# Token halves change roles in the block scheme of the up projection, and the first tile's S1 T1 and A22 T4 are issued early

## The chip, the cores and the metric

The kernel runs on one core of one Trainium2 chip. The metric is the device time of one execution in microseconds (us); the median of three runs before the change is 2224.79 us (2224.76 to 2225.38).

## The reference

Two layers of an encoder trunk on 1024 tokens of width 1024, float32. What matters here is the end of each layer:

```
x  = x + concat(A, B, C) @ W_out
h2 = rmsnorm(x)
up = dwconv3(h2 @ ffn_w_up)            # 1024 -> 2 * 2816
gate, val = split(up)
x  = x + (silu(gate) * val) @ ffn_w_down
```

`A`, `B`, `C` are the outputs of attention, of spatial gating and of a short gated convolution; `dwconv3` is a depthwise convolution over three neighbouring tokens.

## The kernel before

Float32 products are made of three products each: every operand is split into a high part (a rounded copy, on ScalarE) and a low part (the rest, a subtraction on VectorE or GpSimd), and high x high, high x low and low x high are summed in PSUM (`split`, line 114). A product of 128x128 weights with 512 columns is one TensorE instruction; twelve of them (four chunks of the inner dimension, three each) are one *group* (`block_mm`, line 862).

**The up projection** computes 22 tiles (`up_tile`, line 888), each of 128 gate and 128 value channels for all 1024 tokens. A tile is a 2x2 block product by Winograd's scheme with seven products instead of eight. The activations h2 are cut into A11, A12 (two halves of the inner dimension, first 512 tokens) and A21, A22 (the same, last 512 tokens); the weights into B11, B12, B21, B22. From them S1 = A21 + A22, S2 = S1 - A11, S3 = A11 - A21, S4 = A12 - S2 and T1 = B12 - B11, T2 = B22 - T1, T3 = B22 - B12, T4 = T2 - B21 are formed (some with their sign turned). The seven products are A11 B11, A12 B21, S1 T1, S2 T2, S3 T3, S4 B22 and A22 T4. Three of them run on in one PSUM bank u (A11 B11, S2 T2, S3 T3, and A22 T4 behind them), and copies (`cp`, ScalarE) and adds (`add`, line 902, VectorE) take partial sums out of u in between: p1 after the first, u1 after the second. c2 holds A12 B21, c5 holds S1 T1 (copied out as p5) and S4 B22.

**How h2 gets there.** For each of eight blocks of 128 tokens, `norm2_step` (line 815) issues the second half of the output projection (`out_proj`, line 734: five splits on ScalarE and GpSimd, 24 products, and the sum with x on VectorE, line 756), stores x, normalizes the block before (`norm_a`: the square on ScalarE, two short GpSimd operations, the scaling on VectorE at line 262) and issues `norm2_b` (line 770) for the block before that: eight transposes on TensorE into a pair of PSUM banks (line 774), and from there the operand parts. For blocks 0 to 3 these are a copy of both halves (line 783) and the splits of A11 and A12; for blocks 4 to 7 the split of A22, S3 and S2 on VectorE (lines 790, 791) and the two sums for S1 and S4 on GpSimd (lines 792, 793). When all eight blocks are done, `norm2_end` (line 795) splits S2, S1, S3 and S4: ScalarE copies and VectorE subtractions of 128x1024 elements. The PSUM pairs (`big`) are two, of the bank kinds `pa` there are two, of `po` and `pf` one.

**The order.** The program is scheduled by the compiler's expected times (line 1289), except in `manual_schedule` sections, where VectorE, GpSimd and ScalarE keep the written order and TensorE is still scheduled. One such section (lines 1187 to 1205) covers the passage from the last blocks to the first tile. In it, `up_ahead` (line 874) issues A11 B11 and A12 B21 of tiles 0 and 1, which need the first token half alone, while blocks 6 and 7 are still being normalized; `up_prep` (line 845) forms and splits the weights' parts (forming on GpSimd at line 857, the low parts on VectorE or GpSimd at line 117); `up_tile(0)` is a generator that is stepped between them. Tile 2's weights go into the buffers of tile 0's (`up_load`, line 829).

Of the kernel before, what the change touches and what calls it, by code (L numbers as in the profile page):

```python
# [8 lines left out]
F32 = mybir.dt.float32  # L9
# [5 lines left out]
P = 128  # L15
# [19 lines left out]
DRAW = ("H5", "H4")  # L35
# [21 lines left out]
class Trunk:  # L57
# [676 lines left out]
    def out_proj(self, b, half):  # L734
# [21 lines left out]
        nc.vector.tensor_tensor(out=xv, in0=acc, in1=xv, op=ALU.add)  # L756
# [13 lines left out]
    def norm2_b(self, b, xs):  # L770
# [6 lines left out]
        pv = pt.rearrange("p (k t) -> p k t", k=KC)  # L777
        s = slice((b % 4) * P, (b % 4 + 1) * P)
        r0, r1 = self.raw
        if b == 4:  # L780
            self.A["22"] = self.slot(self.xo[0], [2, 4, 512], F32R)
        if b < 4:
            nc.scalar.activation(r0[:, :, s], pv, AF.Copy)
        for n, k in (("11", 0), ("12", 4)) if b < 4 else (("22", 4),):
            h, l = self.A[n][:, 0, :, s], self.A[n][:, 1, :, s]
            self.split(h, l, pv[:, k : k + 4, :], "a", "v")
        if b >= 4:

            a11, a12, s3, s2 = r0[:, 0:4, s], r0[:, 4:8, s], r1[:, 0:4, s], r1[:, 4:8, s]
            nc.vector.tensor_tensor(out=s3, in0=a11, in1=pv[:, 0:4, :], op=ALU.subtract)  # L790
            nc.vector.tensor_tensor(out=s2, in0=pv[:, 4:8, :], in1=s3, op=ALU.subtract)
            nc.gpsimd.tensor_tensor(out=a11, in0=s2, in1=a11, op=ALU.add)
            nc.gpsimd.tensor_tensor(out=a12, in0=a12, in1=s2, op=ALU.subtract)

    def norm2_end(self, names):

        r0, r1 = self.raw
        for n, src, where, els in (
            ("S2", r1[:, 4:8], ("W1", "W4", "Z0", "Z1"), "vv"),
            ("S1", r0[:, 0:4], self.xo[1], "vv"),  # L800
            ("S3", r1[:, 0:4], ("G0", "G2", "G3", "W2"), "vv"),
            ("S4", r0[:, 4:8], ("W5", "G4", "G1", "G5"), "vv"),
        ):
            if n not in names:
                continue
            if isinstance(where, str):
                t = self.A[n] = self.slot(where, [2, 4, 512], F32R)
                for k in (0, 2):
                    self.split(t[:, 0, k : k + 2], t[:, 1, k : k + 2], src[:, k : k + 2], "a", els[k // 2])
            else:  # L810
                t = self.A[n] = [self.S(w, [2, 512], F32R) for w in where]
                for k in range(2):
                    self.split(t[k], t[2 + k], src[:, 2 * k : 2 * k + 2], "a", els[k])
# [59 lines left out]

    def up_ahead(self, f, B):
# [13 lines left out]
    def up_tile(self, f, B, ahead=None, L=None):  # L888
# [4 lines left out]
        if f == 0:  # L893

            self.tmp[0] = self.raw[1].rearrange("p (a b) c -> p a (b c)", a=4)
        elif f == 1:
# [4 lines left out]
        p1, p5, u1 = tg[:, lo], tg[:, hi], tv[:, lo]  # L901
        add = lambda out, ps, sb: nc.vector.tensor_tensor(out=out, in0=ps, in1=sb, op=ALU.add)  # L902
        cp = lambda out, ps: nc.scalar.activation(out, ps, AF.Copy)  # L903
        if ahead:
            u, c2, p1 = ahead
            c5 = self.big()[:, lo] if f == 0 else self.acc("po")
# [386 lines left out]
```

## Time and profile before

| | |
|---|---|
| median of three runs | 2224.79 us |
| profiled execution | 2224.84 us |
| its span, first to last instruction | 2223.0 us |
| TensorE busy | 2202.1 us (99%) |
| VectorE busy | 1507.7 us (68%) |
| ScalarE busy | 1110.9 us (50%) |
| GpSimd busy | 1141.9 us (51%) |
| granted TensorE clock | 0.999 of full |

PE is TensorE, DVE VectorE, ACT ScalarE, POOL GpSimd, and SP issues the transfers. A timeline has a row for each instruction, or for several of one kind in succession: start, time until its end, engine, line, operation, output and inputs by the letters of their buffers, shape and count; in brackets the idle time of the engine before it and what ended it. Products on TensorE overlap, so a row's time is longer than the distance to the next row's start. Since TensorE is nearly always busy, time is to be looked for where it is not, and the two layers pass the same places: the first up tile at about 480 to 510 us and 1581 to 1611 us.

### The profile page before, as it was taken

How to read it: one execution, taken by the hardware profiler on the slowest of the kernel's cores; microseconds unless marked ns; L12 is line 12 of the kernel's file. 1: busy time of each engine (PE TensorE's matmuls, PEld its weight loads, DVE VectorE, ACT ScalarE, POOL GpSimd, SP SyncE). 2: the span in 40 equal slices, each digit the busy share in tenths (PEclk: the TensorE clock that was granted, in tenths of full speed). 3: DMA queues.
4: the chain of work that ended last, by engine and by line, in shares of the span. 5: the costliest groups of instructions: out<-in, count | busy, mean ns of one | idle time of the engine just before them, and what ended most of it. 6: DMA issues, size and time to landing. Idle time of an engine off the chain costs nothing.

```text
span 2223.0 us, 29441 instructions
## 1 busy us (share of the span) xinstructions
PE 2202.1 (99%) x10590; PEld 1828.9 (82%) x10590; DVE 1507.7 (68%) x1949; ACT 1110.9 (50%) x1883; POOL 1141.9 (51%) x1052
## 2 busy tenths in 40 slices
PE   8999999999999999999999999999999999999999
PEld 7888888877888888888888888888788888888887
DVE  5668887178687777854734688862877777778554
ACT  4237776265444444533532477753545454544332
POOL 5564445577777776020143653556776777751100
PEclk9999999999999999999999999999999999999999
DMA  4100002213555453886520000041234545548854
GB/s 157 47 20 1 20 10 95 107 74 109 159 160 169 150 165 118 293 331 204 213 90 10 20 14 7 21 151 57 76 120 155 171 148 166 160 142 322 282 193 163
DMA packets 202020, 281.91 MB, mean 127 GB/s; under 512 B 15598, under 2 KB 121618, under 8 KB 201874
## 3 DMA queue, kind: packets, MB, share of 16 engines
q1 hardware_dynamic: 201874, 280.03, 37.5%
q8 instruction: 83, 1.36, 0.3%
q14 instruction: 63, 0.52, 0.1%
HBM read 199.77 MB, written 80.22 MB: 126 GB/s over the span
## 4 chain that ended last, share of the span: by engine, by line
PE 88%; DVE 4%; DMA 3%; POOL 2%; issue 1%; ACT 1%; SPq 0%; POOLq 0%; DVEq 0%; ACTq 0%
PE pa L869 18%; PE pf L869 8%; PE big L1068 8%; PE pa L1068 5%; PE pa L631 5%; PE pf L301 5%; PE po L869 5%; PE pf L1068 3%; PE po L1068 3%; PE big L615 3%; PE big L614 3%; PE po L643 3%; PE po L644 3%; PE pa L132 2%; PE pa L130 2%; PE pa L131 2%
## 5 line engine op out<-in xcount | busy, mean ns | idle before, releaser
L623 POOL TENSOR_SCALAR H<-H,rv 128x1024 f32<-128x1024 f32 x128 | 144.7, 1132 | 221.5 <-DVE rv L622 221.5
L869 PE MATMUL pa<-H,E 128*128 128x512 f32 x864 | 212.7, 390 | 1.9 <-DVE H L902 1.9
L106 ACT ACTIVATE E<-E 128x512 fp32r<-128x512 f32 (+1 forms) x211 | 132.7, 636 | 163.1 <-POOL E L857 69.7
L636 DVE TENSOR_TENSOR E<-pa,E 128x512 fp32r<-128x512 f32 x256 | 173.4, 688 | 51.9 <-ACT E L635 50.4
L635 ACT ACTIVATE E<-pa 128x512 fp32r<-128x512 f32 x256 | 152.9, 597 | 79.5 <-PE pa L631 78.0
L117 POOL TENSOR_TENSOR E<-E,E 128x512 fp32r<-128x512 f32 x116 | 164.6, 1424 | 52.2 <-ACT E L106 52.2
L869 PEld LDWEIGHTS pa<-H,E 128*128 128x128 f32 x864 | 161.6, 188 | 36.1 <-DVE H L902 2.7
L106 ACT ACTIVATE G<-H 128x1024 fp32r<-128x1024 f32 (+1 forms) x116 | 114.2, 1008 | 141.6 <-PE big L1068 70.9
L117 DVE TENSOR_TENSOR G<-H,G 128x1024 fp32r<-128x1024 f32 (+1 forms) x86 | 100.7, 1173 | 110.4 <-ACT G L106 110.0
L617 DVE TENSOR_REDUCE nm<-big 128x1 f32<-128x1024 f32 x128 | 155.6, 1215 | 8.1 <-PE big L615 8.0
L903 ACT ACTIVATE H<-pa 128x512 f32<-128x512 f32 x128 | 75.9, 593 | 166.2 <-PE pa L869 121.9
L631 PEld LDWEIGHTS pa<-ident,H 128*128 128x128 f32 x1024 | 127.0, 140 | 35.0 <-DVE E L636 1.6
L631 PE MATMUL pa<-ident,H 128*128 128x128 f32 x1024 | 153.7, 272 | 0.0
L620 ACT ACTIVATE H<-big,nm 128x1024 f32<-128x1024 f32 x128 | 142.3, 1112 | 12.3 <-DVE nm L617 12.2
L446 DVE SCALAR_TENSOR_TENSOR big<-H,cst,big 128x1023 f32<-128x1023 f32 x44 | 56.6, 1286 | 106.6 <-ACT big L445 106.6
L117 DVE TENSOR_TENSOR E<-E,E 128x512 fp32r<-128x512 f32 (+1 forms) x96 | 101.4, 1064 | 40.1 <-ACT E L106 40.1
L301 PE MATMUL pf<-H,G 128*128 128x512 f32 x288 | 120.2, 431 | 0.0
L869 PE MATMUL pa<-W,E 128*128 128x512 f32 x336 | 115.0, 391 | 0.3 <-ACT W L106 0.2
L106 ACT ACTIVATE G<-E 128x512 fp32r<-128x512 f32 (+2 forms) x110 | 58.5, 547 | 97.4 <-POOL E L857 26.4
L987 POOL TENSOR_TENSOR E<-E 128x512 f32<-128x512 f32 x26 | 35.3, 1360 | 139.7 <-DMA E<-in_ffn_w_down_dram 139.4
L869 PE MATMUL po<-H,E 128*128 128x512 f32 x408 | 104.3, 389 | 0.0
L857 POOL TENSOR_TENSOR E<-E 128x512 f32<-128x512 f32 x66 | 101.0, 1531 | 3.1
(408 smaller groups left out, 6360.8 us busy)
## 6 DMA issues: line engine op xcount, KB each, us to landing
H<-gdram SPq DMA_DIRECT2D x70, 512.0 KB, 6.0
gdram<-H SPq DMA_DIRECT2D x134, 256.0 KB, 2.3
E<-in_ffn_w_up_dram SPq DMA_DIRECT2D x66, 512.0 KB, 4.4
H<-tdram SPq DMA_DIRECT2D x40, 512.0 KB, 5.0
E<-in_w_in_dram SPq DMA_DIRECT2D x30, 512.0 KB, 3.8
H<-in_ffn_w_down_dram SPq DMA_DIRECT2D x30, 512.0 KB, 4.7
out_dram<-H SPq DMA_DIRECT2D x28, 512.0 KB, 3.1
E<-in_ffn_w_down_dram SPq DMA_DIRECT2D x26, 512.0 KB, 6.0
```

Source lines behind the costliest of these rows:

```text
L106: nc.scalar.activation(out, in_, AF.Copy)
L117: e.tensor_tensor(out=l, in0=src, in1=h.bitcast(F32), op=ALU.subtract)
L301: mm(acc, a[:, k, :], b, start=k + j == 0, stop=k == KC - 1 and j == 2)
L617: nc.vector.tensor_reduce(out=nm, in_=S, op=ALU.max, axis=AX.X, negate=True)
L620: nc.scalar.activation(p, S, AF.Exp, bias=nm, accum_out=sm)
L623: nc.gpsimd.tensor_scalar(out=p, in0=p, scalar1=rv, scalar2=1.0, op0=ALU.mult, op1=ALU.mult)
L631: nc.tensor.transpose(pt[:, r * P : (r + 1) * P], pu[:, r, kc * P : (kc + 1) * P], self.ident)
L635: nc.scalar.activation(hl[:, 0, :], pt, AF.Copy)
L636: nc.vector.tensor_tensor(out=hl[:, 1, :], in0=pt, in1=hl[:, 0, :].bitcast(F32), op=ALU.subtract)
L857: self.nc.gpsimd.tensor_tensor(out=of[t], in0=p, in1=q, op=ALU.subtract)
L869: mm(out, w, x, start=first and k + j == 0, stop=k == 3 and j == 2, skip_group_check=True,)
L1068: nc.tensor.matmul(banks[j], p[:, n, s], r[:, n, :], start=first and n + q == 0 and m < 3, stop=last and n == w - 1 and q == 2, skip_group ...
```

## The change

The token halves change roles: the second half gives A11 and A12, the first half A21 and A22. So S1 and A22 are ready after block 3, and S1 T1 and A22 T4 of the first tile are issued by a new function `up_first` before the last blocks are done; their results are copied out (p5, p7) and added later, so that for tile 0 u ends with S3 T3. A11 B11 and A12 B21 of tiles 0 and 1 now wait for block 7. `norm2_b` is issued ahead of `out_proj` instead of behind it, becomes a generator for blocks 4 to 7, and does all its subtractions on VectorE, from PSUM; S4 lies in the buffer of x. The sum of the last projection (block 7) moves into the hand-written section. The order of the two buffers of the down projection is exchanged. In all tiles the two column halves of `ug` and `uv` are exchanged.

```diff
-DRAW = ("H5", "H4")
+DRAW = ("H4", "H5")
...
     def norm2_alloc(self):
-        self.raw = [self.slot(t, [KC, 512]) for t in self.hreg[0]]
-        self.A = {n: self.slot(t, [2, 4, 512], F32R) for n, t in zip(("11", "12"), self.xreg)}
+        self.raw = self.slot(self.hreg[0][0], [KC, 512])
+        tags = dict(zip(("S1", "22", "12"), (*self.xreg, self.hreg[0][1])))
+        self.A = {n: self.slot(t, [2, 4, 512], F32R) for n, t in tags.items()}
+        self.s4 = self.xt[1][:, 0:2, :].rearrange("p a (k t) -> p k a t", k=4)
...
+        if b < 4:
+            nc.scalar.activation(s3, p0, AF.Copy)
+            self.split(*part("22"), p1, "a", "v")
+            tt(out=s2, in0=p1, in1=s3, op=ALU.add)
+            self.split(*part("S1"), s2, "a", "v")
+            return
         if b == 4:
-            self.A["22"] = self.slot(self.xo[0], [2, 4, 512], F32R)
...
+            self.A["11"] = self.slot(self.xo[0], [2, 4, 512], F32R)
+        for n in order:
+            (ah, al), (bh, bl) = part("11"), part("12")
+            if n in "ab":
+                self.copy("a", *((ah, p0) if n == "a" else (bh, p1)))
             else:
...
+                o, p, q = {
+                    "A": (al, p0, ah.bitcast(F32)), "B": (bl, p1, bh.bitcast(F32)),
+                    "3": (s3, p0, s3), "2": (s2, s2, p0), "4": (s4, p1, s2),
+                }[n]
+                tt(out=o, in0=p, in1=q, op=ALU.subtract)
+            yield
...
     def norm2_step(self, b, xs, g, xout):
-        self.out_proj(b, 1)
-        self.nc.sync.dma_start(xout[b], self.x[b])
+        if b >= 2:
+            rest = self.norm2_b(b - 2, xs[b - 2])
+            for _ in range(7 if b < 7 else 2):
+                next(rest, None)
+        xv, acc = self.out_proj(b, 1, b < 7)
+        if b < 7:
+            self.nc.sync.dma_start(xout[b], self.x[b])
         if b >= 1:
             xs[b - 1] = self.norm_a(b - 1, self.x[b - 1], g, ("G1", "G5"))
-        if b >= 2:
-            self.norm2_b(b - 2, xs[b - 2])
+        return (rest, xv, acc) if b == 7 else None
...
+    def up_first(self, B):
+        self.tmp[0] = self.xt[1]
+        tg = self.tmp[0][:, 2, :]
+        for kind, a, b, o in (("po", "S1", "T1", 512), ("pf", "22", "T4", 0)):
+            c = self.acc(kind)
+            self.block_mm(c, a, B[b], True, True)
+            yield
+            self.nc.scalar.activation(tg[:, o : o + 512], c, AF.Copy)
+            yield
...
+        if f == 0:
+            p7 = p1
             u, c2, p1 = ahead
-            c5 = self.big()[:, lo] if f == 0 else self.acc("po")
+            c5 = self.big()[:, lo]
+            add(ug[:, hi], c2, p1)
+            yield
+            self.block_mm(u, "S2", B["T2"], False, False)
+            add(u1, u, p5)
+            yield
...
+        self.block_mm(u, "S3", B["T3"], False, f == 0)
+        add(uv[:, lo], u, p5)
+        if f == 0:
+            add(ug[:, lo], u, p7)
...
             with self.tc.manual_schedule(engines=MANUAL):
-                xs[7] = self.norm_a(7, self.x[7], g2, ("G1", "G5"))
-                ahead.append(self.up_ahead(0, self.B[0]))
-                self.up_prep(1, raws[1], ("11", "21"))
-                self.norm2_b(6, xs[6])
+                self.up_prep(0, raws[0], ("T4",))
+                b5, xv, acc = late
+                nc.vector.tensor_tensor(out=xv, in0=acc, in1=xv, op=ALU.add)
+                nc.sync.dma_start(xout[7], self.x[7])
+                xs[7], r7 = self.norm_r(7, self.x[7], ("G1", "G5"))
+                for _ in range(3):
+                    next(b5)
+                self.norm_m(xs[7], r7, self.x[7], g2)
+                b6, b7 = self.norm2_b(6, xs[6], "abAB324"), self.norm2_b(7, xs[7], "aAbB324")
+                begun = self.up_first(self.B[0])
+                for steps, n in (
+                    (b5, 2), (b6, 2), (b7, 1), (begun, 1), (b6, 2), (b7, 1), (begun, 1),
+                    (b7, 2), (begun, 2), (b6, 4), (b7, 4),
+                ):
+                    for _ in range(n):
+                        next(steps, None)
+                ahead = [self.up_ahead(0, self.B[0])]
+                self.up_prep(1, raws[1], ("11", "21", "t1"))
+                ahead.append(self.up_ahead(1, self.B[1]))
+                self.up_prep(0, raws[0], ("T2",))
+                self.norm2_end("S2")
                 ahead[0] = self.up_ahead_copy(0, *ahead[0])
-                self.up_prep(0, raws[0], ("T2",))
-                self.norm2_b(7, xs[7])
-                self.up_prep(0, raws[0], ("T3",))
-                ahead.append(self.up_ahead(1, self.B[1]))
+                self.up_prep(0, raws[0], ("T3", "22"))
+                self.up_prep(1, raws[1], ("T1",))
+                self.norm2_end("S3")
+                self.up_prep(1, raws[1], ("t2", "t3"))
                 ahead[1] = self.up_ahead_copy(1, *ahead[1])
-                self.norm2_end(("S2", "S1", "S3"))
+                self.norm2_end("S4")
                 first = self.up_tile(0, self.B[0], ahead[0])
                 next(first)
-                self.up_prep(0, raws[0], ("22", "T4"))
-                self.norm2_end(("S4",))
-                self.up_prep(1, raws[1], ("t1",))
+                self.up_prep(1, raws[1], ("T2",))
                 next(first)
-                self.up_prep(1, raws[1], ("T1", "T2", "T3", "22", "T4"))
+                self.up_prep(1, raws[1], ("T3", "22", "T4"))
```

## Rows read from the trace of the kernel before

**Rows 1.** Busy us by engine in stages: projection, first up tile.

```profile
core 0: us, PE busy (x) PEld busy (x) DVE busy (x) ACT busy (x) POOL busy (x), PEclk, DMA share, GB/s
440.00:480.00 40.00, 40.00 (x200) 33.48 (x199) 24.67 (x27) 23.83 (x53) 34.11 (x47) 1.00 0.20 82
480.00:510.00 30.00, 26.62 (x123) 20.34 (x122) 29.00 (x27) 17.19 (x25) 20.94 (x14) 1.00 0.23 70
```

**Rows 2.** TensorE's waits over the whole span: total us, times, longest.

```profile
PE pa L869 <- DVE Z L117: 4.0, 4, 1.7
...
PE big L869 <- DVE G L117: 2.3, 4, 0.6
PE pa L869 <- DVE H L902: 1.9, 2, 1.3
```

**Rows 3.** Timeline of TensorE, first layer, from block 5's transposes on.

```profile
479.77 1.03 PE L774 MATMUL big<-ident,G 128*128 128x128 f32 x8
480.56 2.99 PE L869 MATMUL pa<-H,E 128*128 128x512 f32 x12
...
493.69 0.51 PE L869 MATMUL pa<-W,E 128*128 128x512 f32 x1 [0.15 <-ACT W L106]
495.85 0.50 PE L869 MATMUL pa<-Z,E 128*128 128x512 f32 x1 [1.65 <-DVE Z L117]
...
508.18 1.41 PE L869 MATMUL big<-G,G 128*128 128x512 f32 x5 [0.56 <-DVE G L117]
509.43 0.62 PE L869 MATMUL po<-H,E 128*128 128x512 f32 x2
509.89 2.88 PE L869 MATMUL pa<-H,E 128*128 128x512 f32 x12
512.61 2.43 PE L869 MATMUL po<-H,E 128*128 128x512 f32 x10
```

**Rows 4.** Timeline of TensorE, second layer, the same place.

```profile
1581.20 1.04 PE L774 MATMUL big<-ident,G 128*128 128x128 f32 x8
...
1614.07 1.29 PE L869 MATMUL po<-H,E 128*128 128x512 f32 x5
```

**Rows 5.** Timeline of VectorE, first layer.

```profile
468.69 1.75 DVE L262 SCALAR_TENSOR_TENSOR G<-H,rsx,E 128x1024 f32<-128x1024 f32 x1 [1.13 <-POOL rsx L125]
...
479.97 0.69 DVE L756 TENSOR_TENSOR H<-po,H 128x512 f32<-128x512 f32 x1
481.48 0.69 DVE L117 TENSOR_TENSOR H<-big,H 128x512 fp32r<-128x512 f32 x1 [0.81 <-ACT H L106]
482.08 0.68 DVE L790 TENSOR_TENSOR H<-H,big 128x512 f32<-128x512 f32 x1
482.79 0.69 DVE L791 TENSOR_TENSOR H<-big,H 128x512 f32<-128x512 f32 x1
483.43 1.28 DVE L262 SCALAR_TENSOR_TENSOR G<-H,rsx,E 128x1024 f32<-128x1024 f32 x1
...
500.22 1.21 DVE L117 TENSOR_TENSOR G<-H,G 128x1024 fp32r<-128x1024 f32 x1
501.36 2.32 DVE L117 TENSOR_TENSOR W<-H,G 128x1024 fp32r<-128x1024 f32 x1
```

**Rows 6.** Timeline of GpSimd, first layer.

```profile
477.48 1.29 POOL L792 TENSOR_TENSOR H<-H,H 128x512 f32<-128x512 f32 x1
...
502.56 2.27 POOL L117 TENSOR_TENSOR E<-E,E 128x512 fp32r<-128x512 f32 x1
```

**Rows 7.** Timeline of ScalarE, first layer.

```profile
480.84 0.60 ACT L106 ACTIVATE H<-big 128x512 fp32r<-128x512 f32 x1 [4.25 <-PE big L774]
481.34 1.05 ACT L256 ACTIVATE G<-H 128x1024 f32<-128x1024 f32 x1
```

**Rows 8.** Timeline of TensorE in the projection: transposes of block 3.

```profile
467.07 1.03 PE L774 MATMUL big<-ident,G 128*128 128x128 f32 x8
```

More of the change, by code (lines that the diff above doesn't have):

```diff
@@ L732, in load_wo1, with out_proj @@
             self.wo1.append((th, tl))
-    def out_proj(self, b, half):
+    def out_proj(self, b, half, add=True):
         nc = self.nc
@@ L755, in out_proj, with norm2_b @@
         xv = self.x[b][:, half * 512 : half * 512 + 512]
-        nc.vector.tensor_tensor(out=xv, in0=acc, in1=xv, op=ALU.add)
+        if add:
+            nc.vector.tensor_tensor(out=xv, in0=acc, in1=xv, op=ALU.add)
+        return xv, acc
     def norm2_alloc(self):
-        self.raw = [self.slot(t, [KC, 512]) for t in self.hreg[0]]
-        self.A = {n: self.slot(t, [2, 4, 512], F32R) for n, t in zip(("11", "12"), self.xreg)}
-    def norm2_b(self, b, xs):
+        self.raw = self.slot(self.hreg[0][0], [KC, 512])
+        tags = dict(zip(("S1", "22", "12"), (*self.xreg, self.hreg[0][1])))
+        self.A = {n: self.slot(t, [2, 4, 512], F32R) for n, t in tags.items()}
+        self.s4 = self.xt[1][:, 0:2, :].rearrange("p a (k t) -> p k a t", k=4)
+    def norm2_b(self, b, xs, order="abA32B4"):
         nc = self.nc
@@ L777, in norm2_b @@
         pv = pt.rearrange("p (k t) -> p k t", k=KC)
+        p0, p1 = pv[:, 0:4, :], pv[:, 4:8, :]
         s = slice((b % 4) * P, (b % 4 + 1) * P)
-        r0, r1 = self.raw
-        if b == 4:
-            self.A["22"] = self.slot(self.xo[0], [2, 4, 512], F32R)
[L782 to L809, printed above, removed]
-            else:
-                t = self.A[n] = [self.S(w, [2, 512], F32R) for w in where]
-                for k in range(2):
-                    self.split(t[k], t[2 + k], src[:, 2 * k : 2 * k + 2], "a", els[k])
@@ new lines, in norm2_end @@
+    def norm2_end(self, n):
+        src, where = {
+            "S2": (self.raw[:, 4:8], ("W1", "W4", "Z0", "Z1")),
+            "S3": (self.raw[:, 0:4], ("G0", "G2", "G3", "W2")),
+            "S4": (self.s4, ("W5", "G4", "G1", "G5")),
+        }[n]
+        t = self.A[n] = [self.S(w, [2, 512], F32R) for w in where]
+        for k in range(2):
+            h, l, v = t[k], t[2 + k], src[:, 2 * k : 2 * k + 2]
+            if n == "S4":
+                h, l = (o.rearrange("p k (a t) -> p k a t", a=2) for o in (h, l))
+            self.split(h, l, v, "a", "v")
@@ L931, in up_tile @@
             self.down_begin(L)
-        self.block_mm(c5, "S4", B["22"], False, True)
-        add(uv[:, lo], c5, u1)
-        self.block_mm(u, "22", B["T4"], False, True)
-        cp(ug[:, hi], u)
+        self.block_mm(c5, "S4", B["22"], f == 0, True)
+        add(uv[:, hi], c5, u1)
+        if f > 0:
+            self.block_mm(u, "22", B["T4"], False, True)
+            cp(ug[:, lo], u)
         cg, cv = self.big(), self.big()
@@ L1177, in run @@
             self.norm2_alloc()
-            ahead, raws, self.tmp = [], {}, [None, None]
+            raws, self.tmp = {}, [None, None]
             self.B, self.formed = {}, {}
             for b in range(NB):
-                self.norm2_step(b, xs, g2, xout)
+                late = self.norm2_step(b, xs, g2, xout)
                 if b == 2:
@@ L1187, in run @@
             with self.tc.manual_schedule(engines=MANUAL):
[L1188 to L1191 removed]
+                self.up_prep(0, raws[0], ("T4",))
+                b5, xv, acc = late
+                nc.vector.tensor_tensor(out=xv, in0=acc, in1=xv, op=ALU.add)
+                nc.sync.dma_start(xout[7], self.x[7])
```

39 lines of the change are left out of this document (18 added, 21 removed).

## The prediction, made before the changed kernel was run

> **What bounds the kernel now.** I read the stage table first, then the waits of TensorE, then the timelines of the engines around the place of the change. In the stage before it (output projection, second half) TensorE is busy for all of its 40 us; in the 30 us behind it (first up tile) it is busy for 26.62 while VectorE is busy for 29.00 [rows 1]. Over the whole run TensorE's largest named waits are for VectorE in this stage, 4.0 and 2.3 us over two layers, and 1.9 us later at line 902 [rows 2]. So the kernel is bound by TensorE, and the only thing that this change can give is the loss at the first up tile of each layer.
>
> That loss is larger than the named waits. In the first layer the transposes of block 5 start at 479.77, and at 512.61 the last ten products of tile 1's S1 T1 (two of them ran before): 32.84 us [rows 3]. A group of 12 products takes 2.72 us (509.89 to 512.61) and eight transposes 0.79 (479.77 to 480.56, where the next row starts). Done in between are three times eight transposes (2.37), nine groups (24.48) and two products (0.45), 27.3 us. **The loss is 5.5 us a layer**; the second layer runs from 1581.20 to 1614.07, 32.87 us [rows 4], so 11.1 us in all, 0.5% of the run. It can't give more than that, but for the 1.9 us of line 902.
>
> VectorE makes this loss. From the sum of block 7 at 479.97 it works through all operand parts, S4's last, and TensorE's S4 products wait for its end until 508.18 [rows 3, 5]. Its passes are slow because GpSimd runs beside it: a 128x1024 pass with two SBUF inputs takes 1.21 us where VectorE has the start, and 2.32 us where GpSimd has; GpSimd's 128x512 pass takes 1.29 alone and 2.27 behind VectorE [rows 5, 6]. The two take turns, a whole instruction each: a pass of GpSimd costs VectorE 2.32 - 1.21 = 1.1 us. Passes that read PSUM are not drawn out: they start 0.60 apart, 0.71 where one needs the one before (481.48, 482.08, 482.79) [rows 5].
>
> **The change part by part.** I keep the clock of the first layer. All durations are of the profiled execution, 2224.84 us, which is 0.05 above the median of the runs shown.
>
> Blocks 0 to 3: the copy of both halves becomes one of a half, A22 is split where A11 and A12 were, S1 is formed and split. ScalarE does no more than before; VectorE has one pass more for each block, the low part of S1, with two SBUF inputs, so it takes turns with GpSimd: 4 x 0.6 = 2.4 us of GpSimd's time, which has 40 - 34.11 = 5.9 idle [rows 1]. Cost nothing, hidden by TensorE's full stage; if that cover is gone, up to 2.4 us a layer.
>
> Blocks 4 to 7: GpSimd loses its eight sums (lines 792, 793), VectorE has five passes for each block instead of three, ScalarE two copies instead of one. The transposes of block 5 go ahead of the last projection (0.79 us moved, none added), so the projection ends at 480.56 and VectorE's sum of block 7, which is now the first of the hand-written order, starts at about 480.8. VectorE's queue from there, in the order written:
> - the sum 0.6, three passes of block 5: 483.2. From the sum to the scaling of block 7 (line 262) it took 3.46 us, of which 0.5 was the squaring waiting for a copy on ScalarE [rows 5, 7]; that copy is gone, so the scaling starts at 483.7 and takes 1.2: 484.9;
> - two passes of block 5, which free the PSUM pair for block 7's transposes: 486.1; two of block 6: 487.3;
> - block 7's transposes 0.8 and its first copy 0.6 on ScalarE [rows 7] hold A11's low part until 487.7; two more ScalarE copies hold A12's, which ends at 489.3;
> - six passes for S3, S2, S4 of blocks 6 and 7, 3.8: 493.1; low parts of tile 1's B11 and B21 and of tile 0's T2, 0.6 each: 494.9;
> - S2's first low part, 1.15: 496.0. By now GpSimd has four passes ready (22 of tile 0, T1 of tile 1, and forming t2 and t3), as it waits only for copies of ScalarE that stand behind S2's. So S2's second part, T3, S3's two and S4's first come in turns: 1.15 + 0.6 + 3 x 1.15 for VectorE and 4 x 1.1 for GpSimd: S4's first part ends at 505.6;
> - S4's second 506.8, the add of c2 507.4, a turn of GpSimd until 507.9, T2 of tile 1 508.5, **the add of u1 509.1**. S3 T3 goes into the bank that u1 is read from, so it is queued behind this add.
>
> TensorE meanwhile: from 480.56 transposes of block 6, S1 T1, A22 T4, transposes of block 7: 480.56 + 1.58 + 5.44 = 487.6. A11 B11 needs block 7's low part, 488.35: 0.8 idle. Five groups (A11 and A12 of both tiles, S2 T2) bring it to 502.0. Here it has nothing: u of both tiles, po and pf are held, the free PSUM pair is c5's and waits for S4 until 505.6, 3.6 idle; S4 B22 until 508.3, S3 T3 from 509.1 (0.8 idle, or filled by tile 1's S1 T1, as po is free at 507.4) to 511.8. Together 4.4 to 5.2 us idle, and 0.2 for the slow first product behind each wait (495.85 stands 2.16 behind 493.69, with 1.65 named and 0.23 the product's own [rows 3]). The nine groups end at about 512.0; before, 512.61 less the two products, 512.16. **The change gives 0.15 us a layer, 0.3 in all**: the early products fill the wait for the second half, and VectorE's longer queue brings the wait back behind S2.
>
> The rest: the other tiles swap the halves that sums are written to, the same passes. The copies of S1 T1 and A22 T4 are ScalarE's, which is busy 17.19 of 30 us [rows 1]. The store of block 7 is issued by SP behind the moved sum, at most 0.8 later, and nobody reads it soon. Tile 2's weights can be loaded earlier, since the passes of GpSimd that free their buffers (the second from 502.56 to 504.83 [rows 6]) now run at 498 and before: this could take the 1.9 us of line 902 [rows 2] or leave them; I bound it by 1.9 either way and take 0. The swapped order of the buffers for the down projection follows A11's and S1's new places; it frees its first buffer one group earlier, and I take 0.
>
> Sum: 2224.84 - 0.3 = 2224.5.
>
> **The rivals.** A measurement of this kernel can tell about 0.2%, 4.4 us, from no change.
>
> A, *VectorE is not held by GpSimd* (faster). If the four GpSimd passes fall elsewhere, say because ScalarE's copies for them come later than S3's, the 4 x 1.1 us go: S4's first part is there at 501.2, the add of u1 at 504.1, and TensorE's only wait is the 0.8 for block 7: S4 B22 from 502.0, S3 T3 until 507.4, 4.6 us a layer before the 512.16 of now. Time: 2224.84 - 9.2 = 2215.6; with two of the four turns gone 2220.2. For it: the eight sums are gone from GpSimd, 1.29 us and more each. Against: the four passes are ready just then, as before's pass was that followed VectorE's at 502.56 [rows 6]. The Trainium skill, GPSIMD Engine Reference, section Engine selection, says that elementwise work belongs on VectorE, being about twice as slow on GpSimd; by that rule moving the sums is a gain as such, and A's time would be the result. The rows agree on the ratio (1.29 against 0.60), but here VectorE is the engine that is late.
>
> B, *transposes wait ahead of the projection* (slower). A block's transposes (and copies) now stand in the program before the projection of two blocks later, not behind it. Block 4's would take the place of block 3's at 467.07 [rows 8], but its scaling ends at 468.69 + 1.75 = 470.44 [rows 5]: 3.4 us of wait in a stage that is bound by TensorE, in each layer: 2224.84 + 6.8 - 0.3 = 2231.3. It decides from the point where TensorE reaches them before 470.4; each product of the projection that the scheduler slips in ahead takes 0.23 off. Against: the scheduler orders by the times that it expects, and before there was no wait in this stage [rows 1].
>
> C, *S3 T3 is placed before S4 B22*. Then TensorE waits from 502.0 to 509.1 and S4 follows: nine groups end at 514.5, 2.4 us later a layer: 2224.84 + 4.8 = 2229.6. Against: in the expected times S4 is ready first.
>
> D, *it doesn't do what it says*: the scheduler puts the two early groups late. Then 5.4 us open up before A11 B11, and the groups fill the 4.4 us behind S2 T2 instead: 1.0 us a layer worse, 2226.5.
>
> **How the numbers follow.** Forecast 0.52 (2221 to 2228, with the 1.9 and with the last wait filled or not), A 0.24, B 0.13, C 0.09, D 0.02. Of A all but a little lies more than 0.2% lower, with a tail of the forecast 0.27; of B and C 0.17 lies more than 0.2% higher, with the forecast's upper tail 0.19; same is the rest, 0.54. The range takes in A down to its end and all but the upper part of B: 2215.5 to 2230.
>
> **What would show it.** Right: S1 T1 and A22 T4 of tile 0 right behind the last projection; one wait under 1.5 us before A11 B11; VectorE busy without a gap to about 509; a wait of 3 to 4 us between S2 T2 and S4 B22, released by a low part of S4. Wrong: S4's passes at 1.2 us each (A); waits at the transposes in the projection stage (B); the long wait released by line 902's add (C). The forecast falls if the span differs by over 5 us.

## The result, and the profile of the changed kernel

The changed kernel takes 2233.09 us (median of 4 runs, 2232.08 to 2234.67) beside 2224.78 us before (4 runs): ratio 1.0043, 95% interval 1.0030 to 1.0055. It is slower by 8.3 us, where 0.3 us faster was forecast and 2230 was the end of the range. The profiled execution took 2232.08 us, its span is 2230.1.

The stage table of the changed kernel answers to [rows 1]; two short stretches are added. Columns as there.

```profile
440.00:480.00 40.00, 39.66 (x200) 33.11 (x199) 27.49 (x33) 24.33 (x57) 33.39 (x43) 1.00 0.20 80
480.00:510.00 30.00, 24.25 (x108) 19.30 (x107) 28.06 (x29) 16.59 (x26) 15.03 (x9) 0.95 0.22 70
506.00:511.00 5.00, 4.27 (x12) 3.37 (x13) 5.00 (x5) 0.00 (x0) 4.37 (x3) 0.66 0.00 0
1607.00:1613.00 6.00, 1.74 (x4) 1.46 (x5) 6.00 (x5) 1.59 (x3) 4.74 (x3) 0.73 0.28 82
```

In the first up tile TensorE is now busy for 24.25 us instead of 26.62, and the granted clock falls to 0.95 there; in the five us from 506 on it is 0.66, and in the second layer 0.73 from 1607 on. Before, the first up tile had 1.00 [rows 1].

The timeline of TensorE, first layer, answers to [rows 3]; its first row is in the projection, the others follow the last projection product (478.96):

```profile
464.68 1.06 PE L784 MATMUL big<-ident,G 128*128 128x128 f32 x8 [0.34 <-DVE G L262]
...
479.19 2.89 PE L888 MATMUL pf<-H,E 128*128 128x512 f32 x12
481.92 1.04 PE L784 MATMUL big<-ident,G 128*128 128x128 f32 x8
482.71 3.01 PE L888 MATMUL po<-H,E 128*128 128x512 f32 x12
485.56 1.03 PE L784 MATMUL big<-ident,G 128*128 128x128 f32 x8
487.28 0.50 PE L888 MATMUL pa<-H,E 128*128 128x512 f32 x1 [0.69 <-ACT H L106]
488.00 2.77 PE L888 MATMUL pa<-H,E 128*128 128x512 f32 x11 [0.22 <-DVE H L812]
...
501.50 0.39 PE L888 MATMUL big<-W,E 128*128 128x512 f32 x1
506.73 0.50 PE L888 MATMUL big<-G,E 128*128 128x512 f32 x1 [4.84 <-DVE G L117]
...
509.07 0.63 PE L888 MATMUL pa<-W,E 128*128 128x512 f32 x1
509.50 0.63 PE L888 MATMUL pa<-Z,E 128*128 128x512 f32 x1
...
511.41 2.89 PE L888 MATMUL po<-H,E 128*128 128x512 f32 x12
```

The two early groups stand right behind the projection (479.19, 482.71). Then there is a short wait before A11 B11 and one of 4.84 us in S4 B22, released by S4's low part. Behind it the products stand 0.43 us apart (509.07, 509.50) where 0.227 is usual: that is the lower of the two clock levels, 1.2 GHz. The 13 products from 506.73 to 511.41 take 4.68 us instead of 2.95. TensorE's timeline in the second layer repeats this, with more of it at half clock: the 13 products from 1611.26 to 1616.78 take 5.52 us.

```profile
1611.26 0.79 PE L888 MATMUL big<-G,E 128*128 128x512 f32 x1 [4.83 <-DVE G L117]
...
1616.78 2.91 PE L888 MATMUL po<-H,E 128*128 128x512 f32 x12
```

VectorE's timeline, first layer, answers to [rows 5]:

```profile
478.45 1.53 DVE L262 SCALAR_TENSOR_TENSOR G<-H,rsx,E 128x1024 f32<-128x1024 f32 x1
479.91 0.68 DVE L1226 TENSOR_TENSOR H<-po,H 128x512 f32<-128x512 f32 x1
...
487.26 0.69 DVE L812 TENSOR_TENSOR H<-big,H 128x512 fp32r<-128x512 f32 x1 [0.81 <-ACT H L106]
...
492.45 0.69 DVE L812 TENSOR_TENSOR H<-big,H 128x512 f32<-128x512 f32 x1
493.06 1.28 DVE L117 TENSOR_TENSOR E<-E,E 128x512 fp32r<-128x512 f32 x2
494.26 1.78 DVE L117 TENSOR_TENSOR G<-E,G 128x512 fp32r<-128x512 f32 x1
495.96 3.45 DVE L117 TENSOR_TENSOR Z<-H,W 128x1024 fp32r<-128x1024 f32 x2
499.34 1.77 DVE L117 TENSOR_TENSOR G<-E,G 128x512 fp32r<-128x512 f32 x1
501.04 2.30 DVE L117 TENSOR_TENSOR G<-H,G 128x1024 fp32r<-128x1024 f32 x1
503.26 2.28 DVE L117 TENSOR_TENSOR W<-H,G 128x1024 fp32r<-128x1024 f32 x1
505.46 1.21 DVE L117 TENSOR_TENSOR G<-H,W 128x1024 fp32r<-128x1024 f32 x1
```

GpSimd's timeline, first layer, answers to [rows 6]:

```profile
493.82 1.68 POOL L876 TENSOR_TENSOR E<-W,E 128x512 f32<-128x512 f32 x1 [11.08 <-DVE E L117]
496.06 4.51 POOL L117 TENSOR_TENSOR E<-E,E 128x512 fp32r<-128x512 f32 x2 [0.56 <-ACT E L106]
500.65 1.61 POOL L876 TENSOR_TENSOR E<-W,E 128x512 f32<-128x512 f32 x1
502.22 2.24 POOL L876 TENSOR_TENSOR W<-W 128x512 f32<-128x512 f32 x1
```

S4's first low part, VectorE's last row above, ends at 506.67. GpSimd has five passes in a row beside VectorE's last passes, and before them nothing for 11.08 us: the forming of tile 1's t1 waits for VectorE's split of that tile's B11 (493.06).

**Where the time went.** From 479.19 to 519.13, the end of S3 T3, there are 39.94 us, in which 11 groups of 2.72 and 16 transposes (1.58) are done: 8.4 us lost, 5.5 before. Counted between products, the wait before A11 B11 is 1.4, that in S4 B22 5.0 (506.73 - 501.50 - 0.23), the half clock 1.7 (4.68 - 2.95). In the second layer the same stretch loses 9.3, of which 2.6 are half clock. Comparing the starts of equal-numbered TensorE products in the two traces, the changed kernel also falls back by 0.5 us in each of the two projection stages, where eight transposes now wait for VectorE's scaling (0.34 us at 464.68, 0.36 at 1569.19), and by some 1.1 in all elsewhere. The spans differ by 7.1 us only, since the profiled execution of before lost 1.9 us in its first 40 us, where its granted clock was 0.85 between 20 and 30 us and the changed kernel's 1.00, with the same instructions. So times read off these two traces can't be set side by side as they stand. The stage of the kernel before:

```profile
20.00:30.00 10.00, 10.00 (x43) 8.16 (x43) 3.80 (x7) 4.87 (x11) 3.97 (x8) 0.85 0.45 154
```

### The profile page after: what moved, and what is told of

It is laid out like the page before. It is cut to its first block, busy times and chain, and to the rows that moved or that the text cites. A ratio compares the mean times of both kernels' runs of the same rounds, so it can differ in the third digit from the quotient of the medians.

```text
span 2230.1 us, 29424 instructions
## 1 busy us (share of the span) xinstructions
PE 2202.9 (99%) x10590; PEld 1831.2 (82%) x10590; DVE 1517.1 (68%) x1973; ACT 1106.5 (50%) x1885; POOL 1121.6 (50%) x1036
## 4 chain that ended last, share of the span: by engine, by line
PE 88%; DVE 4%; POOL 3%; DMA 2%; issue 1%; ACT 1%; SPq 0%; POOLq 0%; DVEq 0%; ACTq 0%
PE pa L888 19%; PE pf L888 9%; PE big L1104 8%; PE pa L1104 5%; PE po L888 5%; PE pa L631 5%; PE pf L301 5%; PE pf L1104 3%; PE po L1104 3%; PE big L615 3%; PE big L614 3%; PE po L643 3%; PE po L644 3%; PE pa L130 2%; PE pa L131 2%; PE pa L132 2%
## 5 line engine op out<-in xcount | busy, mean ns | idle before, releaser
L888 PE MATMUL pa<-H,E 128*128 128x512 f32 x840 | 207.2, 390 | 4.4 <-DVE H L930 2.6
L117 POOL TENSOR_TENSOR E<-E,E 128x512 fp32r<-128x512 f32 x118 | 169.8, 1444 | 55.9 <-ACT E L106 55.9
L117 DVE TENSOR_TENSOR G<-H,G 128x1024 fp32r<-128x1024 f32 (+1 forms) x86 | 105.7, 1231 | 110.0 <-ACT G L106 109.6
L888 PE MATMUL po<-H,E 128*128 128x512 f32 x432 | 109.8, 389 | 0.0
L888 PE MATMUL pa<-W,E 128*128 128x512 f32 x320 | 109.7, 390 | 0.0
```

Of the source, the lines that this page charges most:

```text
L117: e.tensor_tensor(out=l, in0=src, in1=h.bitcast(F32), op=ALU.subtract)
L888: mm(out, w, x, start=first and k + j == 0, stop=k == 3 and j == 2, skip_group_check=True,)
```

## The experiments

The theory after the first reading, W: what sets the time is VectorE's queue up to S4's first part, drawn out by turns with GpSimd; the change leaves TensorE one unbroken wait there, and behind it the clock falls. Against it stood R1 (the loss sits in the projection or later), R2 (the wait alone, without the clock), R3 (GpSimd doesn't hold VectorE) and R4 (the half clock belongs to the changed order, whatever the waits). All ten kernels below were timed beside the kernel before; its median was 2224.11 us in the first set, 2223.83 in the second, 2223.26 in the third.

**1. S4 ahead of S3 in VectorE's queue.**

```diff
-                self.up_prep(0, raws[0], ("T3", "22"))
+                self.up_prep(0, raws[0], ("22",))
                 self.up_prep(1, raws[1], ("T1",))
-                self.norm2_end("S3")
-                self.up_prep(1, raws[1], ("t2", "t3"))
+                self.norm2_end("S4")
                 ahead[1] = self.up_ahead_copy(1, *ahead[1])
-                self.norm2_end("S4")
                 first = self.up_tile(0, self.B[0], ahead[0])
                 next(first)
+                self.up_prep(0, raws[0], ("T3",))
+                self.norm2_end("S3")
+                self.up_prep(1, raws[1], ("t2", "t3"))
                 self.up_prep(1, raws[1], ("T2",))
                 next(first)
```

> The changed kernel with S4's split, and the add of c2 behind it, moved ahead of T3's and S3's splits in the hand-written order; nothing is left out. Theory W (the loss is one unbroken wait of TensorE for S4's first low part, 5.0 us a layer counted between products, plus TensorE at half clock behind it, 1.7 us in the first layer and 2.6 in the second): S4's first low part is ready about 6 us earlier, before S2 T2 ends; the wait of 4.8 us is gone, the granted clock stays full, and the time falls by about 5.0 + 1.7 + 5.0 + 2.6 = 14.3 us less some 1 us of new short waits: 2220 us (2217 to 2223), below the kernel before. Rival R1 (the loss lies in the projection stage and in the later tiles, through the new order of transposes): the time stays near 2233 us. Rival R2 (the wait alone is the loss, the half clock would come anyway): 2223 us with half-clock products left.

Measured: 2228.81 us, ratio 1.0022 (1.0013 to 1.0031). The 4.84 us wait is gone, with 0.81 and 0.57 left of it, but a new one stands behind it in TensorE's timeline:

```profile
511.46 0.72 PE L888 MATMUL pa<-W,E 128*128 128x512 f32 x2 [1.99 <-DVE E L117]
```

The stretch at it in the stage table:

```profile
511.00:516.00 5.00, 4.54 (x13) 3.61 (x14) 3.29 (x5) 1.02 (x2) 5.00 (x4) 0.66 0.29 87
```

Tile 1's S2 T2 now waits for its T2, whose low part stood behind S3's two passes, and the clock falls behind this wait too. In the second layer the same wait of 1.99 us (1616.16) was followed by full clock. A third of the gain expected came, because the order was mended in one place and late in the next.

**2. Three GpSimd passes later.** T1, t2 and t3 of tile 1 are written behind S4's split.

```diff
-                self.up_prep(1, raws[1], ("T1",))
                 self.norm2_end("S3")
-                self.up_prep(1, raws[1], ("t2", "t3"))
                 ahead[1] = self.up_ahead_copy(1, *ahead[1])
                 self.norm2_end("S4")
+                self.up_prep(1, raws[1], ("T1",))
+                self.up_prep(1, raws[1], ("t2", "t3"))
```

> The changed kernel with GpSimd's work for T1 and the forming of t2 and t3 of tile 1 moved behind S4's split in the hand-written order; nothing is left out. Theory W (VectorE's passes with two SBUF inputs and GpSimd's passes take turns, 1.1 us each): three of the four turns ahead of S4's first low part go, so it is ready 3.3 us earlier, TensorE's wait falls from 4.8 to about 1.5 us and the half clock goes: 2233.1 - 2 x 3.3 - 4.3 = 2222 us (2220 to 2226). Rival R2 (wait alone): 2226.5 with half clock left. Rival R3 (GpSimd does not hold VectorE; the queue is late by its own length): S4's passes stay where they were, 2233 us.

Measured: 2229.66 us, ratio 1.0023 (1.0014 to 1.0033). GpSimd's queue has nothing else, so it ran on with these passes as soon as their inputs stood there, and they still met VectorE's. GpSimd's timeline:

```profile
501.41 1.44 POOL L117 TENSOR_TENSOR E<-E,E 128x512 fp32r<-128x512 f32 x1 [2.52 <-ACT E L106]
502.93 2.12 POOL L876 TENSOR_TENSOR E<-W,E 128x512 f32<-128x512 f32 x1
```

One turn fewer lay ahead of the end of S4's first part, which came 13.13 us behind the start of VectorE's last pass from PSUM instead of 14.22 (506.67 - 492.45): one turn is worth 1.1 us, as the prediction had it. The wait was 3.75, and the half clock stayed (granted clock 0.50 from 505 to 511 us). The expectation of 2222 us missed, since one turn went instead of three. R3 doesn't fit the turn that went, and experiment 6 tests it again; moving a pass in the written order is not moving it in time.

**3. TensorE kept busy in the wait.** Sixteen products that nothing reads, 3.6 us of extra work, stand between S2 T2 and S4 B22.

```diff
+            h, _ = self.a_op("S4", 0)
+            for _ in range(16):
+                nc.tensor.matmul(idle, B["22"][:, 0, 0, :], h, start=True, stop=True)
```

> The changed kernel with 16 products of no use (3.6 us of TensorE, into the idle half of c5's PSUM pair) between S2 T2 and S4 B22 of tile 0 in each layer. S4's low part comes when it came, so the end of the wait is not moved. Theory W: the unbroken wait is cut to about 1.4 us, the granted clock stays full behind it, and the time falls by what the half clock cost, 1.7 + 2.6 = 4.3 us: 2228.8 us (2227 to 2231). Rival R2 (the half clock is no matter of the wait, or costs nothing): 2233 us.

Measured: 2230.56 us, ratio 1.0033 (1.0022 to 1.0045), 2.5 us below the changed kernel, with intervals that overlap. TensorE's timeline (line 943 are the added products):

```profile
501.69 3.79 PE L943 MATMUL big<-W,E 128*128 128x512 f32 x16
506.96 0.50 PE L888 MATMUL big<-G,E 128*128 128x512 f32 x1 [1.26 <-DVE G L117]
...
511.48 2.58 PE L888 MATMUL po<-H,E 128*128 128x512 f32 x10 [0.88 <-DVE H L930]
```

S4 B22 goes on at nearly the same place, 506.96 for 506.73, but at full clock: no stretch of either first tile is below it. In the first layer's stage table, with the granted clock third from the end:

```profile
500.00:520.00 20.00, 17.77 (x76) 13.72 (x75) 18.11 (x15) 6.80 (x13) 17.95 (x12) 1.00 0.28 79
```

A wait of 0.88 for an add took part of the gain back. That useless work made the kernel faster is likely, but the times alone don't show it; that it kept the clock, the rows do. So the half clock follows from TensorE's pause and not from the order: R2 and R4 are out.

**4. The pause put into the kernel before.** S4's first low part is computed three times there, two 128x1024 passes of VectorE as extra work.

```diff
                     self.split(t[k], t[2 + k], src[:, 2 * k : 2 * k + 2], "a", els[k])
+                    if n == "S4" and k == 0:
+                        for _ in range(2):
+                            self.nc.vector.tensor_tensor(
+                                out=t[2], in0=src[:, 0:2], in1=t[0].bitcast(F32), op=ALU.subtract
+                            )
```

> The kernel before with S4's first low part computed three times (the same values; two more 128x1024 passes of VectorE, 2.3 us each beside GpSimd). Theory W: TensorE's wait for S4 grows from 0.56 to about 5.1 us in one piece; behind it the granted clock falls to half for 3.4 to 6.8 us, so each layer loses 4.6 + 1.7 to 2.6 us: 2224.8 + 13.5 = 2238 us (2236 to 2241). Rival R2 (a wait costs its own length): 2224.8 + 9.2 = 2234 us, clock full. Rival R4 (the half clock belongs to the changed kernel's other order, not to a wait): clock full here.

Measured: 2232.54 us, ratio 1.0039 (1.0026 to 1.0053); the expectation was 5.5 us too high, and by the time alone R2's 2234 would fit better. The scheduler put A22 T4 ahead of S4 B22, so that this group stands in the pause, waiting for an add behind the first of the two added passes. TensorE's timeline, second layer:

```profile
1612.12 4.61 PE L874 MATMUL pa<-H,E 128*128 128x512 f32 x12 [3.38 <-DVE H L907]
```

Twelve products take 4.61 us behind the 3.38 us wait, where 2.9 is usual: the fall comes in the kernel before too, once it has such a pause. The first layer doesn't show this: there A22 T4 waited 1.65 us, with full clock behind it, and the clock had fallen earlier, from 496 us on, behind a wait of 1.66 that the kernel before has too.

**5. Experiment 1 with tile 1's T2 ahead of T3 and S3.** Against experiment 1:

```diff
                 next(first)
-                self.up_prep(0, raws[0], ("T3",))
-                self.norm2_end("S3")
                 self.up_prep(1, raws[1], ("t2", "t3"))
                 self.up_prep(1, raws[1], ("T2",))
                 next(first)
+                self.up_prep(0, raws[0], ("T3",))
+                self.norm2_end("S3")
```

> The first run's order (S4's split ahead of S3's), with one change: tile 1's t2, t3 and the split of its T2 now stand behind S4 and ahead of T3 and S3, so that the 1.99 us wait at tile 1's S2 T2 should go. Theory W (one unbroken wait of TensorE, made by VectorE's queue and its turns with GpSimd, and the half clock behind it): no TensorE wait over 1 us between the last projection product and the end of the first tile, no half clock in the first tile of either layer, the first tile 3 to 4 us shorter a layer than in the changed kernel: 2225 (2222 to 2228). R1 (the loss sits in the projection or in later tiles): 2229 to 2233, as the first run. R4 (the half clock belongs to the changed order whatever the waits): half clock again, 2228 or more.

Measured: 2222.02 us, ratio 0.9994 (0.9985 to 1.0003). The waits of TensorE from 476 to 575 us are these, with no half clock in either first tile:

```profile
PE big L888 <- DVE G L117: 1.4, 2, 0.8
PE pa L888 <- ACT H L106: 0.7, 1, 0.7
PE pa L888 <- DVE H L812: 0.2, 1, 0.2
```

The order of a few instructions, most of them in VectorE's queue, gives back the whole loss of 8.3 us and leaves the kernel level with the one before. R1 is out as the main loss.

**6. Tile 1's weights in GpSimd's idle 11 us.** B11 and B21 of tile 1 are split on GpSimd, early, and T1, t2, t3 follow; VectorE's order stays.

```diff
-                early = f < 2 and n in ("11", "21")
-                B[n] = self.up_split(of[n], "v" if early or n in ("11", "T2", "T3") else "p")
+                early = f < 1 and n in ("11", "21")
+                B[n] = self.up_split(of[n], "v" if early or n in ("T2", "T3") or n == "11" and f != 1 else "p")
...
-                    (b5, 2), (b6, 2), (b7, 1), (begun, 1), (b6, 2), (b7, 1), (begun, 1),
-                    (b7, 2), (begun, 2), (b6, 4), (b7, 4),
+                    (b5, 2), (b6, 2), ("11", "21"), (b7, 1), (begun, 1), (b6, 2), (b7, 1), (begun, 1),
+                    (b7, 2), (begun, 2), ("T1", 0), (b6, 4), (b7, 4),
                 ):
+                    if isinstance(steps, str):
+                        self.up_prep(1, raws[1], (steps, n) if n == "21" else (steps, "t2", "t3"))
+                        continue
...
-                self.up_prep(1, raws[1], ("11", "21", "t1"))
...
-                self.up_prep(1, raws[1], ("T1",))
...
-                self.up_prep(1, raws[1], ("t2", "t3"))
```

> The changed kernel with tile 1's weights made early: its B11 and B21 are split on GpSimd instead of VectorE, behind block 6's first two copies, and T1, t2 and t3 of tile 1 follow, in the 11 us in which GpSimd has nothing to do and VectorE's passes read PSUM; the order of VectorE's passes is otherwise the changed kernel's (S2, T3, S3, S4). Theory W: VectorE loses two passes (1.3 us) and four turns (1.1 us each) ahead of S4's first low part, which then ends about 5 us earlier, near 501.5, when S2 T2 ends: the 4.84 us wait falls under 1 us and the half clock behind it goes; first tile 6 to 7 us shorter a layer; 2220 (2217 to 2224), at or below the kernel before. R3 (GpSimd does not hold VectorE, its pass was only late for its own products): S4 comes 1.3 us earlier and the wait stays above 3 us: 2229 to 2233. R1 (loss elsewhere): not below 2229.

Measured: 2223.65 us, ratio 0.9997 (0.9988 to 1.0006). The 4.84 us wait became 0.64, and 0.87 at another place in TensorE's timeline:

```profile
503.12 1.42 PE L888 MATMUL big<-G,E 128*128 128x512 f32 x5 [0.64 <-DVE G L117]
505.41 3.02 PE L888 MATMUL po<-H,G 128*128 128x512 f32 x12 [0.87 <-DVE H L930]
```

R3 would have left a wait of over 3 us.

**7. The transposes back behind the projection.** As before the change:

```diff
     def norm2_step(self, b, xs, g, xout):
-        if b >= 2:
-            rest = self.norm2_b(b - 2, xs[b - 2])
-            for _ in range(7 if b < 7 else 2):
-                next(rest, None)
         xv, acc = self.out_proj(b, 1, b < 7)
...
         if b >= 1:
             xs[b - 1] = self.norm_a(b - 1, self.x[b - 1], g, ("G1", "G5"))
+        if b >= 2:
+            rest = self.norm2_b(b - 2, xs[b - 2])
+            for _ in range(7 if b < 7 else 2):
+                next(rest, None)
```

> The changed kernel with block b-2's transposes and passes back behind block b's projection, as the kernel before has them. Theory W: this placement costs 0.6 us in the first layer's projection and 0.35 in the second's (the lag of the work-aligned traces), so 2232.2 (2230.5 to 2234), and the wait of nearly 5 us for S4 stays. R1 (the loss sits in the projection stage): back to 2226 or less. Rival B of the prediction (transposes that hold the projection up, 3 us a layer): 2226 to 2228.

Measured: 2233.68 us, ratio 1.0042 (1.0029 to 1.0054). TensorE is busy for all of the 40 us from 440 on again, so the 0.5 us of the projection comes back; but the transposes of block 7 then wait in TensorE's timeline:

```profile
487.56 1.06 PE L784 MATMUL big<-ident,G 128*128 128x128 f32 x8 [0.68 <-DVE H L812]
```

The wait for S4 behind it is 4.81 us. The move is worth nothing that this measurement can tell, either way, and neither rival B nor R1 comes back.

**8. S1 T1 and A22 T4 not early, first try.** Both are issued among tile 1's first products, in a PSUM pair of their own.

```diff
-        for kind, a, b, o in (("po", "S1", "T1", 512), ("pf", "22", "T4", 0)):
-            c = self.acc(kind)
+        two = self.big()
+        for a, b, o in (("S1", "T1", 512), ("22", "T4", 0)):
+            c = two[:, o : o + 512]
...
-                    (b5, 2), (b6, 2), (b7, 1), (begun, 1), (b6, 2), (b7, 1), (begun, 1),
-                    (b7, 2), (begun, 2), (b6, 4), (b7, 4),
+                    (b5, 2), (b6, 2), (b7, 1), (b6, 2), (b7, 3), (b6, 4), (b7, 4),
...
                 self.norm2_end("S2")
+                for _ in begun:
+                    pass
```

> The changed kernel with S1 T1 and A22 T4 of the first tile not early: they stand behind A12 B21 and among tile 1's first products, so that the transposes of blocks 6 and 7 follow the last projection product at once. One more split of tile 2 lands ahead of S3 in VectorE's queue. Theory W (TensorE has to wait for S4's first part in any case, and the early products only move an idle time from ahead of A11 to ahead of S4): TensorE idles some 5 us ahead of A11 B11, block 7's transposes come 1.4 us earlier, and the two products (5.5 us) fill the wait for S4, which falls to 2 us or less: first tile the same or up to 3 us shorter a layer, 2229 (2225 to 2233). Rival (the early products are worth the 5.5 us of TensorE's time that they fill ahead of A11): 2240 or more.

Measured: 2257.07 us, ratio 1.0151 (1.0137 to 1.0165), far above the range of W. The number would fit the rival, which said 2240 or more, but the rows show another cause. The edit put the two copies out of PSUM ahead of the copies for T3, S3 and S4 in ScalarE's queue, and a split of tile 2 ahead of both. ScalarE's timeline:

```profile
503.68 0.63 ACT L106 ACTIVATE E<-E 128x512 fp32r<-128x512 f32 x1 [8.14 <-PE pf L888]
...
508.29 0.60 ACT L903 ACTIVATE H<-big 128x512 f32<-128x512 f32 x1 [3.10 <-PE big L888]
```

ScalarE stands for 8.14 and 3.10 us, and VectorE behind it. So the run decides neither for W nor for the rival; it shows what a copy that waits for TensorE costs in a queue that everything passes.

**9. The same with one copy behind S4's.**

```diff
                 self.norm2_end("S2")
+                next(begun)
...
                 self.norm2_end("S4")
+                next(begun, None)
```

> S1 T1 and A22 T4 not early once more, now with one copy of both products behind S4's copies in ScalarE's queue, so that no copy of VectorE's passes stands behind them (in the run before, S3's and S4's copies did). Theory W (VectorE's queue to S4's first part sets the time, and the early products only move an idle time of TensorE from ahead of S4 to ahead of A11): TensorE idles 5 to 6 us ahead of A11 B11, the two products fill the wait for S4, S4 B22 begins within 1.5 us of the changed kernel's place: 2233 (2229 to 2237). Rival (the early products are worth the 5.5 us a layer that they fill ahead of A11): 2242 or more.

Measured: 2234.93 us, ratio 1.0052 (1.0039 to 1.0065). TensorE's timeline:

```profile
485.14 1.94 PE L784 MATMUL big<-ident,G 128*128 128x128 f32 x8 [4.20 <-DVE H L812]
487.77 4.71 PE L888 MATMUL pa<-H,E 128*128 128x512 f32 x12 [0.69 <-ACT H L106]
...
508.66 0.39 PE L888 MATMUL big<-W,E 128*128 128x512 f32 x1
508.88 0.39 PE L888 MATMUL big<-G,E 128*128 128x512 f32 x1
```

The idle time is back ahead of A11 B11 (4.20 and 0.69, and the half clock follows it there: a row of 12 products takes 4.71, where 2.9 is usual), and there is none at S4 B22. Two groups issued early, 5.4 us of TensorE's work a layer, changed the time by 1.8 us in all, 2234.93 against 2233.09, with intervals that overlap. The rival, which said 2242 or more, is out: issued early, the two groups only moved the idle time to another place. W held in the time, but not in all: S4 B22's second product came 30.2 us behind the last projection product (478.72 here), where it was 27.8 in the changed kernel (478.96 to 506.73), and not within 1.5 us of it. S4's first part ended at 507.22, before TensorE came to it, so in this run the idle time ahead of A11 B11 and the half clock behind it make the loss, and not S4.

**10. Orders 5 and 6 together.** Weights of tile 1 early on GpSimd; behind S2 on VectorE S4, c2's add, tile 1's T2, then T3 and S3. To the edit of experiment 6 comes

```diff
-                self.up_prep(0, raws[0], ("T3", "22"))
-                self.norm2_end("S3")
+                self.up_prep(0, raws[0], ("22",))
+                self.norm2_end("S4")
                 ahead[1] = self.up_ahead_copy(1, *ahead[1])
-                self.norm2_end("S4")
                 first = self.up_tile(0, self.B[0], ahead[0])
                 next(first)
                 self.up_prep(1, raws[1], ("T2",))
                 next(first)
+                self.up_prep(0, raws[0], ("T3",))
+                self.norm2_end("S3")
```

> The changed kernel with both orders together: tile 1's weights early on GpSimd, and behind S2 on VectorE first S4's split, c2's add, the split of tile 1's T2, and only then T3 and S3. Theory W: each of the two left one or two short waits (0.8 and 0.6 us for S4 with the one, 0.6 and 0.9 us with the other); together no TensorE wait over 0.5 us between A11 B11 and the end of the first tile, no half clock there, the first tile 3 us shorter a layer than in the kernel before: 2220 (2217 to 2223), below both. R1 (later tiles give it back): 2223 to 2226, as either order alone.

Measured: **2215.88 us (7 runs), ratio 0.9971 (0.9960 to 0.9983)**, 7.4 us faster than the kernel before and some 17 faster than the changed one, 1 us beyond the range expected. The stage table from 480 on:

```profile
480.00:510.00 30.00, 29.31 (x137) 23.95 (x136) 27.65 (x30) 18.12 (x29) 17.32 (x13) 1.00 0.22 70
```

VectorE's timeline:

```profile
483.94 2.48 DVE L812 TENSOR_TENSOR H<-big,H 128x512 fp32r<-128x512 f32 x4
...
496.41 2.22 DVE L117 TENSOR_TENSOR G<-H,W 128x1024 fp32r<-128x1024 f32 x1
```

GpSimd's timeline:

```profile
484.67 2.52 POOL L117 TENSOR_TENSOR E<-E,E 128x512 fp32r<-128x512 f32 x2 [1.97 <-ACT E L106]
```

TensorE is busy for 29.31 of 30 us, and 0.69, ahead of A11 B11, is its only wait there. S4's first part ends at 498.6 (496.41 + 2.22) instead of 506.67, before S2 T2 does. VectorE's four passes that read PSUM and GpSimd's two beside them keep their own times, 0.62 and 1.26 each: there was a place where GpSimd costs VectorE nothing, and the change had left it empty.

## Why the prediction was wrong

**What held.** The loss before was in the first up tile. The two groups went to the place given; VectorE had only short gaps (28.06 us busy of 30); the wait between S2 T2 and S4 B22 was there and was released by S4's low part, though 4.84 us long and not 3 to 4; S4 B22 stood ahead of S3 T3 (rival C did not come); rival B came at a tenth of its size, as the transposes that wait for the scaling in the projection waited 0.34 and 0.36 us and not 3.4; the early groups were early (rival D did not come). Also its main sentence held: the early products fill the wait for the second half, and VectorE's longer queue brings the wait back behind S2. Experiment 9 shows the other side: with these products late, the idle time is ahead of A11 B11 and none is left at S4.

**The step that failed** is "Together 4.4 to 5.2 us idle, and 0.2 for the slow first product behind each wait". It counts only the time in which TensorE stands. The products behind the wait ran at half clock, for which the sum has no term: 1.7 us in the first layer and 2.6 in the second, 4.3 of the 8.6 us by which the forecast missed. The kernel before has waits of at most 1.7 us at this place [rows 2] and no fall there, so the rows chosen did not show it; experiments 3 and 4 do. But its trace had a fall elsewhere, in the first 40 us, where the granted clock was 0.85 from 20 to 30 us behind a wait of 1.74 us; the prediction made no use of it. It also passed over that stretch in its list of waits: 2.7 us in all at line 280, between the 4.0 and the 2.3 that it names.

**The terms that were mis-sized.** These are told for the first layer. The wait for S4: 5.0 instead of 3.6 in each layer, 2.8 in all. From the end of the projection, 480.56 in the prediction and 479.19 in the trace, S4's first part ended after 27.5 us and not 25.0, 2.4 late, while TensorE reached the wait 0.9 late. Of the 2.4, 1.1 is a turn: GpSimd had five passes for turns and not four, since forming t1 of tile 1 (493.82) fell in the same stretch; the queue had left it out. The other 1.3 were lost ahead of the turns. VectorE's sum of block 7 (479.91) began 0.7 us behind the projection's end and not 0.2, as the scaling of block 6 was still running (478.45, 1.53 us). And A11's low part of block 7 (487.26) came 8.1 us behind it and not 7.1; here the prediction disagrees with itself: its TensorE sum ends block 7's transposes at 487.6 and the copy takes 0.6, but it starts the low part at 487.7.

The wait before A11 B11, for the same copy and low part: 1.4 instead of 0.8, 1.2 in all. The projection: 1.0, costed at nothing. These come to 5.0; with the half clock 9.3, and with some 1.1 elsewhere 10.4. On the other side stand the 0.8 us a layer ahead of S3 T3, which the forecast counted and tile 1's S1 T1 filled. That leaves 8.8, against the 8.6 missed.

**Rival A** asked whether GpSimd holds VectorE. It does, at the price given. The sign that the prediction gave for A, S4's passes at 1.2 us each, half came without A: S4's first part took 1.21 us, as the turns fell on the passes ahead of it. The Trainium skill, GPSIMD Engine Reference, section Engine selection, sends elementwise work to VectorE, by which moving the sums off GpSimd should have gained as such. No run moved the sums alone, so this isn't tested by itself; but here VectorE is the late engine, and experiment 6, which moved two splits the other way, onto an engine that is slower at them, and had GpSimd work on T1, t2 and t3 of tile 1 earlier, came out 9.4 us below the changed kernel.

What stays open: why the changed kernel loses some 1.1 us outside the projection and the first tiles was not tried. What it loses in the projection, undoing the one move (experiment 7) gave back and lost again behind. And why the clock fell behind some waits of 1.6 to 2 us and not behind others, no run shows.

## What to carry to other kernels

When the late engine is not the one that is full, filling the full engine's idle time early gave nothing here: shorten the late engine's queue instead, by putting first in it what is waited for first, and by giving its neighbour the work while the late engine's passes read PSUM. A written order that looks late may still run early, and a helper's pass that waits for one instruction of the late engine can make it idle for 11 us and collide afterwards. And a wait of TensorE has to be priced with what runs behind it, not by its length alone.

## What the runs showed of the hardware

The granted clock of TensorE falls from 2.4 to 1.2 GHz for a few us behind a pause: products stood 0.43 us apart instead of 0.227. It came behind waits of 4.84, 4.83, 4.20, 3.75 and 3.38 us, and in experiment 1 once behind 1.99 us, while the same 1.99 us in the other layer of the same execution was followed by full clock. In experiment 4 it came behind 1.66 us too (granted clock 0.57 from 496 to 500 us); the kernel before has that wait, 1.65, and keeps 1.00 behind it [rows 1] [rows 3]. So it differs between places that look alike. Keeping TensorE at work in the pause, even with products that nobody reads, kept the clock at 1.00 in experiment 3.
